# A hybrid decoder layer on one core: the columns in use found from sums of the picks' weights on GpSimd, in place of count products on TensorE

## The chip, the core and the metric

One core of a Trainium2 chip. Its engines run side by side, each through its own queue in program order: TensorE (PE, with the loading of weights listed as PEld), VectorE (DVE), ScalarE (ACT), GpSimd (POOL) and SyncE (SP), which here only issues transfers. The metric is the time of one execution on the device in microseconds (us), the median of the runs. One more execution was recorded by the hardware profiler; every row of a trace comes from that one.

## What is computed

A decoder layer on 256 tokens of width 1024: two attention mixers, their merge, and behind them the part that matters here, a PEER channel mixer. For every token it scores 128 + 128 keys in each of 8 heads, picks the best 16 pairs of a head, and so 128 of 16384 experts with softmax weights. Cut to this part:

```
s = einsum('thcd,cnd->thcn', q, subkeys)          # q = norm(x) @ w_q
s1, i1 = top_k(s[:, :, 0], 16); s2, i2 = top_k(s[:, :, 1], 16)
sc, ci = top_k((s1[..., :, None] + s2[..., None, :]).reshape(T, H, 256), 16)
idx = i1[ci // 16] * 128 + i2[ci % 16];  g = softmax(sc)
a = einsum('td,thkd->thk', x, u[idx])
out = einsum('thk,thkd->td', gelu(a) * g, v[idx])
```

## The kernel before

The kernel does not gather rows of u. It lays the 16384 experts out as 128 columns of 128 experts (partition p, column e) and multiplies all of them with the tokens, column by column; the products of one column are a tile of 128 experts by 256 tokens, and the table of all columns is A (`A1`, `A2`). Then it multiplies A by the softmax weights, of which all but the picked ones are zero, and multiplies the result with v.

**The stage of u.** A loop over e from 0 to 127 takes one column a step. `take()` issues the weights' load (four raw buffers), ScalarE rounds a tile to its high part (`hi_to`, L141) and VectorE subtracts that to get the low part (`lo_to`, L149); both run two or three columns ahead. TensorE does 24 products (`mm3`, L175 to L177), three for each of eight pieces. After every second column `u_evac` applies the GELU on ScalarE (L1091, L1094); where the weights of some tokens stand in A already, its result goes to a work buffer `w0`, and GpSimd multiplies it into A (L1096). At the end of every step `vector_work` does a piece of side work. First that is `select`, the top-k on VectorE. When that is done, it is the groups: `RATE` is 1.15, so a step does one group of four tokens, and about every seventh step two.

**A group** is spread over three steps by `groups_step`. `one_hots` makes on VectorE a one-hot of the pick's partition (L1037, named oh), a one-hot of its column (L1037, eq), and the latter times the weight in two 16-bit parts (L1039). Two groups later `gate_mm` multiplies them on TensorE: for each of four tokens two products into the gate tile `gp` in PSUM (L1047) and one more, the count product, into `used` (L1048), which stays in PSUM over all 64 groups and sums up the high parts of the weights of every expert, apart for tokens 0 to 127 and 128 to 255. A step later `gate_evac` takes the gates out of PSUM: for columns that have their products already VectorE multiplies them into A (L1077, one input in PSUM, one in SBUF), for the others ScalarE copies them to A (L1079), behind VectorE's part since both write A.

**Behind the groups** `lists` runs in small pieces of `yield`ed cost beside the last columns. L1137 makes a flag of every expert in `used` (sum above zero); the flags are sorted into a list of up to 98 slots a partition, by VectorE's max and replace operations on the first level, 32 small matmuls (L1173), and a second level. The indices (L1179) drive the gathers of v's rows and of A's rows on GpSimd (L1284) in the last stage (`v_mm`, L1267). Finished columns of A go to memory through SP (`a_write`, L1056), which the gathers wait for. If the list has no room, a flag makes a branch at the end do the rest.

Order: each engine does its instructions in the order in which the program writes them; TensorE, VectorE, ScalarE and GpSimd wait for each other through the tiles they share. Tiles of one name share a ring of buffers (`w0` has two).

Of the kernel before, what the change touches and what calls it, by code (L numbers as in the profile page):

```python
# [9 lines left out]
F32 = mybir.dt.float32  # L10
F32R = mybir.dt.float32r
BF16 = mybir.dt.bfloat16
# [3 lines left out]
AF = mybir.ActivationFunctionType  # L16
OP = mybir.AluOpType
AX = mybir.AxisListType
PSUM = bass.MemoryType.PSUM

S, D, HD = 256, 1024, 64
KT = D // 128
NT = S // 128
# [4 lines left out]
NH, NK, TOPK = 8, 128, 16  # L28
# [22 lines left out]
NW = NK - ND  # L51
# [51 lines left out]
def tile_hybrid_nsa_dilated_peer(ctx, tc, x, win, wgate, consts, gains, gcols, n1g, n2g, pe, w1, w2, wun, wud, wo, wq, subk,  # L103
                                 cpos, pu, pv, out):
    nc = tc.nc
# [4 lines left out]
    RAW, GT = 4, 4  # L110
# [187 lines left out]
    hT = norm_T(work, x1, g1, None, first_split, psQ, "S")  # L298
    tok = lambda T, k, t: (T[0][:, k, t * 128:(t + 1) * 128], T[1][:, k, t * 128:(t + 1) * 128])

# [93 lines left out]
    def rope(q4, at, bt, nh, np_):  # L394

        T = q4.shape[1]
        a = work.tile([128, T, nh, 16], F32, name="ra")
        b = work.tile([128, T, nh, 16], F32, name="rb")
        a, b = a[:np_], b[:np_]
        bc = lambda z: z.unsqueeze(2).to_broadcast([np_, T, nh, z.shape[-1]])  # L400
        nc.gpsimd.tensor_tensor(a, q4[:, :, :, 0:16], bc(at), op=OP.mult)
# [283 lines left out]
    for t in range(NT):  # L685
        for g in range(3):
            for par in range(2):
                dil_units.append(Unit(
                    ("d%d" % g, t), t, [par, par + 2], 4, {"dq%d" % g, "dk%d" % g, "dv%d" % g},
                    lambda h, g=g: dqT[hrow(h), g, h // 2, :], lambda h, g=g: dkT[hrow(h), g, h // 2, :],  # L690
                    lambda h, k, g=g: vD[:, k, g, h * 64:h * 64 + 64],
# [155 lines left out]
    octx.close()  # L847
    gctx = ExitStack()
    psG = gctx.enter_context(tc.tile_pool(name="psG", bufs=1, space=PSUM))

    used = psG.tile([128, NT, NK], F32, name="used")
    mctx.close()


# [5 lines left out]
    tp_ = ctx.enter_context(tc.tile_pool(name="tp", bufs=2))  # L860
    iotah = tp_.tile([128, NK], F16, name="iotah", bufs=1)

    zero = tp_.tile([128, 2 * S], F32, name="w0")
    nc.gpsimd.memset(zero[0:1], 0.0)
    for o in range(0, ad.shape[1], 2 * S):
# [16 lines left out]
    def Ae(e, n, t0=0, t1=S):  # L882
        return A1[:, e:e + n, t0:t1] if e < 96 else A2[0][:, e - 96:e - 96 + n, t0:t1]
# [8 lines left out]
    for h in range(0, NH, 2):  # L892
        p = psP.tile([128, 2, S], F32, name="pj")
# [131 lines left out]

    prog = {"T": 0, "C": 0}

# [13 lines left out]
        return o1, o2  # L1041

    def gate_mm(t0, oh):
        p = psG.tile([128, GT, NK], F32, name="gp", bufs=3)
        for j in range(GT):
            for i in range(2):
                nc.tensor.matmul(p[:, j, :], oh[0][:, j, :], oh[1][:, j, i, :], start=(i == 0), stop=(i == 1))  # L1047
            nc.tensor.matmul(used[:, t0 // 128, :NW], oh[0][:, j, :], oh[1][:, j, 0, :NW], start=(t0 == 0 and j == 0),  # L1048
                             stop=(t0 == S - GT and j == GT - 1), skip_group_check=True)
        return p  # L1050

    writes = []
# [1 line left out]
    def a_write(e, n, t0, t1):  # L1054
        def f():
            nc.sync.dma_start(ad[e * 128:(e + n) * 128, D + t0:D + t1].rearrange("(e p) t -> p e t", p=128), Ae(e, n, t0, t1))  # L1056
        writes.append((n * (t1 - t0) // 2, f))
# [11 lines left out]
    def gate_evac(t0, p):  # L1069

        pt = p.rearrange("p t e -> p e t")
        C = prog["C"]
        for lo_, hi_ in ((0, 96), (96, 128)):
            m = min(max(C, lo_), hi_)
            if m > lo_:
                av = Ae(lo_, m - lo_, t0, t0 + GT)
                nc.vector.scalar_tensor_tensor(av, pt[:, lo_:m, :], 1.0 / GSCALE, av, op0=OP.mult, op1=OP.mult)  # L1077
            if hi_ > m:
                nc.scalar.activation(Ae(m, hi_ - m, t0, t0 + GT), pt[:, m:hi_, :], AF.Copy, scale=1.0 / GSCALE)  # L1079
        T = prog["T"] = t0 + GT  # L1080
        if T % 128 == 0:
            n = 4 if T < S else 6
            for z in ((0, min(C, 96)), (96, min(C, NW))):
                for e in range(*z, n):
                    a_write(e, min(n, z[1] - e), T - 128, T)
# [30 lines left out]
    def groups_step(n):  # L1116

        for _ in range(n):
            ps = [(t0, gate_mm(t0, oh)) for t0, oh in q_oh[:1]] if len(q_oh) == 2 or state.get("end") else []
            if ps:  # L1120
                q_oh.pop(0)
            for t0, p in q_ps:
                gate_evac(t0, p)
            q_ps[:] = ps
            t0 = next(groups, None)
            if t0 is None:
                state["end"] = True
            else:
                q_oh.append((t0, one_hots(t0)))
# [4 lines left out]
    def lists():  # L1134

        fl = tp_.tile([128, NT, NK], F32, name="oh1", bufs=3)
        nc.vector.tensor_scalar(fl[:, :, :NW], used[:, :, :NW], 0.0, None, op0=OP.is_gt)  # L1137
        yield 300
        kk = tp_.tile([128, 2, NK], F32, name="oh1", bufs=3)
        di = tp_.tile([128, 2, 128], F32, name="oh1", bufs=3)  # L1140
        idm = tp_.tile([128, 2, 128], F32, name="eq", bufs=1)
        nc.gpsimd.iota(idm[:, 0, :], pattern=[[128, 128]], base=-int(PAD), channel_multiplier=1,
                       allow_small_or_imprecise_dtypes=True)
        nc.gpsimd.tensor_copy(di, ident.unsqueeze(1).to_broadcast([128, 2, 128]))
        cols = lambda z: z[:, :NW]
        u0, u1, ids = cols(fl[:, 0, :]), cols(fl[:, 1, :]), cols(idm[:, 0, :])
        k, s_ = kk[:, 0, :NW], kk[:, 1, :NW]

        nc.vector.tensor_scalar(k, u0, -2.0, 1.0, op0=OP.mult, op1=OP.add)
        nc.vector.tensor_tensor(k, k, u1, op=OP.mult)  # L1150
        nc.vector.scalar_tensor_tensor(k, u0, 3.0, k, op0=OP.mult, op1=OP.add)
        yield 550
        nc.vector.scalar_tensor_tensor(s_, k, 0.5, ids, op0=OP.is_gt, op1=OP.mult)
        nc.vector.tensor_scalar(k, k, PAD / KEY, KEY, op0=OP.add, op1=OP.mult)
        nc.vector.tensor_tensor(k, k, s_, op=OP.add)
        yield 550
        for level in range(2):

            for a, b in ((0, 64), (64, NW)) if level == 0 else ((0, NW),):
                kp = k[:, a:b]  # L1160
                for r in range(a, b, 8):
                    nc.vector.max(s_[:, r:r + 8], kp)
                    if r + 8 < b:
                        nc.vector.match_replace(out=kp, in_to_replace=s_[:, r:r + 8], in_values=kp, imm_value=PAD)
                    yield 260 + 3.5 * (b - a)
            yield 3500
            if level == 0:

                p = psTr.tile([128, NW], F32, name="tr")
                d2 = di.rearrange("p a b -> p (a b)")  # L1170
                for j in range(16):
                    o = (128 - 5 * j) % 128
                    nc.tensor.matmul(p[:, j:NW:16], d2[:, o:o + 128], s_[:, j:NW:16], start=True, stop=True)  # L1173
                nc.scalar.activation(k, p, AF.Copy)
                yield 2000
        ei = tp_.tile([128, 4, 128], I32, name="eT", bufs=1)
        idx["a"] = ei[:, 0, :]
        nc.vector.tensor_copy(ei[:, 2, :NW], s_)
        nc.vector.tensor_scalar(ei[:, 0, :NW], ei[:, 2, :NW], int(KEY) - 1, None, op0=OP.bitwise_and)  # L1179
        yield 1300  # L1180

        c = fl[:, 0, 0:1]
        nc.vector.tensor_scalar(c, s_[:, CAPC:CAPC + 1], PAD + 0.5, None, op0=OP.is_gt)
        nc.vector.scalar_tensor_tensor(c, s_[:, CAP0:CAP0 + 1], 2.0 * KEY, c, op0=OP.is_ge, op1=OP.add)
        nc.vector.scalar_tensor_tensor(c, s_[:, S1 - 1:S1], 3.0 * KEY, c, op0=OP.is_lt, op1=OP.add)
        yield 2600
        p = psTr.tile([1, 1], F32, name="tr")
        nc.tensor.matmul(p, c, mhalf, start=True, stop=True)
        nc.vector.tensor_scalar(ei[0:1, 3, 0:1], p, -0.25, None, op0=OP.is_lt)
        idx["more"] = ei[0:1, 3, 0:1]  # L1190
        yield 300

    mk = lists()

    def list_work(ns):
# [38 lines left out]
    for e in range(NK):  # L1234
        if e % 2 == 0:
            p = psP.tile([128, 2, S], F32, name="pj")
# [259 lines left out]
```

## Time and profile before

| | us |
|---|---|
| median of 3 runs (975.61 to 978.22) | 975.74 |
| the profiled execution | 977.78 |
| its span, first to last instruction | 975.93 |
| TensorE busy | 955.8 (98%) |
| VectorE busy | 725.5 (74%) |
| ScalarE busy | 501.0 (51%) |
| GpSimd busy | 264.4 (27%) |

Shares over the whole span are averages over stages of different kinds; what a change in one stage is worth is read from that stage. The columns of rows are said in front of each group of them below. In all of them "out<-in" are the names of the program's tiles, and L and a number is the line. A recorded matmul's duration includes its way through the array, and matmuls overlap; VectorE's records overlap their neighbours by some 0.1 us as well.

### The profile page before, as it was taken

The numbers are of one execution on the slowest core, as the hardware profiler recorded it, in microseconds if no ns is written. First come the engines' busy times: TensorE is split into PE (matmuls) and PEld (weight loads), VectorE is DVE, ScalarE is ACT, GpSimd is POOL, SyncE is SP. The second block draws the span as 40 slices with busy tenths as digits, with TensorE's granted clock in tenths as the row PEclk, the third lists the DMA queues.
The fourth block names the chain that finished last, engine by engine and source line by source line (L and its number), as shares of the span: only waits on it lengthen the run. The fifth ranks groups of instructions, "written<-read, shape, count | busy, mean of one in ns | idle before, by whom it ended". The sixth has DMA issues, their size and how long they took to land.

```text
span 975.9 us, 18699 instructions
## 1 busy us (share of the span) xinstructions
PE 955.8 (98%) x7163; PEld 887.0 (91%) x7163; DVE 725.5 (74%) x1471; ACT 501.0 (51%) x866; POOL 264.4 (27%) x272
## 2 busy tenths in 40 slices
PE   9999999999999999998999999999999989999997
PEld 9989898998889999998999999999998868888885
DVE  5587666556667898899888999997664657777775
ACT  6466634444445445445544444434344546766663
POOL 4412224000000141041000011112123867666620
PEclk9999999999999999999999999999899999999999
DMA  8879755559776789888878778856898999999941
GB/s 283 290 249 326 266 173 196 187 202 349 273 247 238 242 306 314 302 301 301 299 259 267 259 196 244 234 166 198 264 302 288 403 409 320 327 327 329 323 148 46
DMA packets 95638, 259.91 MB, mean 266 GB/s; under 512 B 9908, under 2 KB 39221, under 8 KB 95543
## 3 DMA queue, kind: packets, MB, share of 16 engines
q1 hardware_dynamic: 80566, 193.25, 60.0%
q0 software_dynamic: 14112, 64.23, 18.0%
q8 instruction: 58, 0.95, 0.4%
q10 hardware_dynamic: 864, 1.18, 0.4%
q14 instruction: 38, 0.30, 0.1%
HBM read 240.80 MB, written 80.75 MB: 329 GB/s over the span
## 4 chain that ended last, share of the span: by engine, by line
PE 88%; DVE 8%; issue 2%; ACT 1%; POOL 1%; DMA 0%; ACTq 0%; POOLq 0%
PE acc L1267 24%; PE pj L175 17%; PE pj L177 16%; PE pj L176 16%; PE gp L1047 3%; DVE lo L149 3%; PE pv L593 2%; PE S L549 2%; PE used L1048 1%; PE tr L577 1%; PE tr L910 1%; DVE oh L980 1%; PE acc L177 1%; PE acc L175 1%; PE acc L176 1%
## 5 line engine op out<-in xcount | busy, mean ns | idle before, releaser
L175 PE MATMUL pj<-T_h,hi 128*128 128x256 f32 x1104 | 319.0, 289 | 0.5 <-ACT A L1091 0.4
L177 PE MATMUL pj<-T_h,lo 128*128 128x256 f32 x1104 | 313.7, 284 | 2.9 <-DVE lo L149 2.8
L176 PE MATMUL pj<-T_l,hi 128*128 128x256 f32 x1104 | 312.9, 283 | 0.0
L149 DVE TENSOR_TENSOR lo<-raw,hi 128x1024 fp32r<-128x1024 f32 x204 | 259.5, 1275 | 50.0 <-PE pj L177 26.7
L141 ACT ACTIVATE hi<-raw 128x1024 fp32r<-128x1024 f32 x205 | 216.4, 1060 | 156.2 <-PE pj L176 58.2
L177 PEld LDWEIGHTS pj<-T_h,lo 128*128 128x128 f32 x1104 | 212.2, 192 | 4.7 <-DVE lo L149 4.5
L175 PEld LDWEIGHTS pj<-T_h,hi 128*128 128x128 f32 x1104 | 212.3, 192 | 1.9 <-ACT A L1091 0.6
L176 PEld LDWEIGHTS pj<-T_l,hi 128*128 128x128 f32 x1104 | 212.4, 192 | 0.0
L1284 POOL DMA_INDIRECT A<-ad,eT x98 | 131.9, 1346 | 60.3 <-DVE oh L1228 33.1
L1267 PE MATMUL acc<-hi,w 128*128 128x512 f32 x336 | 131.0, 390 | 2.9 <-issue 1.6
L1267 PE MATMUL acc<-lo,w 128*128 128x512 f32 x336 | 130.8, 389 | 0.0
L1267 PE MATMUL acc<-hi,oh 128*128 128x512 f32 x336 | 130.8, 389 | 0.0
L1323 DVE TENSOR_TENSOR lo<-A,hi 128x1024 fp32r<-128x1024 f32 x98 | 119.5, 1219 | 0.0
L1096 POOL TENSOR_TENSOR A<-A,w 128x512 f32<-128x512 f32 (+28 forms) x39 | 39.1, 1003 | 256.2 <-ACT w L1094 256.2
L1290 ACT ACTIVATE hi<-A 128x1024 fp32r<-128x1024 f32 x98 | 102.6, 1047 | 6.2 <-DMA A<-ad,eT 6.2
L175 PE MATMUL pj<-hi,T_h 128*128 128x256 f32 x336 | 97.1, 289 | 0.0
L1228 DVE TENSOR_TENSOR oh<-A,w 128x256 fp32r<-128x256 f32 x106 | 44.8, 423 | 70.3 <-ACT w L1227 62.7
L176 PE MATMUL pj<-lo,T_h 128*128 128x256 f32 x336 | 95.2, 283 | 0.3 <-DVE lo L149 0.3
L177 PE MATMUL pj<-hi,T_l 128*128 128x256 f32 x336 | 95.1, 283 | 0.0
L1227 ACT ACTIVATE w<-A 128x256 fp32r<-128x256 f32 x106 | 44.1, 417 | 77.9 <-PE acc L1267 74.8
L1267 PEld LDWEIGHTS acc<-hi,w 128*128 128x128 f32 x336 | 63.1, 188 | 16.9 <-issue 2.1
L1267 PEld LDWEIGHTS acc<-hi,oh 128*128 128x128 f32 x336 | 63.1, 188 | 13.4 <-DVE oh L1228 0.3
(276 smaller groups left out, 1421.3 us busy)
## 6 DMA issues: line engine op xcount, KB each, us to landing
raw<-in_pu_dram SPq DMA_DIRECT2D x128, 512.0 KB, 4.5
ad<-in_pv_dram SPq DMA_DIRECT2D x120, 512.0 KB, 5.8
raw<-in_win_dram SPq DMA_DIRECT2D x44, 512.0 KB, 4.5
ad<-A SPq DMA_DIRECT2D x27, 256.0 KB, 4.9
ad<-A SPq DMA_DIRECT2D x17, 384.0 KB, 6.0
raw<-in_w_dram SPq DMA_DIRECT2D x8, 512.0 KB, 4.4
raw<-in_wo_dram SPq DMA_DIRECT2D x8, 512.0 KB, 5.2
raw<-in_wq_dram SPq DMA_DIRECT2D x8, 512.0 KB, 4.5
```

The costliest lines, as they stand in the source:

```text
L141: nc.scalar.activation(split[i], raws[i], AF.Copy)
L149: nc.vector.tensor_tensor(lo, raws.pop(i), split[i], op=OP.subtract)
L175: nc.tensor.matmul(ps, s_[0], m_[0], start=first, stop=False, skip_group_check=True)
L176: nc.tensor.matmul(ps, s_[0], m_[1], start=False, stop=False, skip_group_check=True)
L177: nc.tensor.matmul(ps, s_[1], m_[0], start=False, stop=last, skip_group_check=True)
L1096: nc.gpsimd.tensor_tensor(av, av, tmp[:, :, :T], op=OP.mult)
L1227: nc.scalar.activation(wh, a, AF.Copy)
L1228: nc.vector.tensor_tensor(wl, a, wh, op=OP.subtract)
L1267: nc.tensor.matmul(acc[t][d], w[w_][:, ts_], v[v_][:, d * 512:(d + 1) * 512], start=(t, d) not in begun, stop=last and n == 2, skip_group_ ...
L1284: nc.gpsimd.indirect_dma_start(out=b, out_offset=None, in_=ad, in_offset=bass.IndirectOffsetOnAxis(ap=idx["a"][:, s_:s_ + 1], axis=0))
L1290: nc.scalar.activation(hi, raw, AF.Copy)
L1323: nc.vector.tensor_tensor(lo, v_of(n_lo), his[n_lo], op=OP.subtract)
```

## The change

The count products go, and the tile `used` moves from PSUM to SBUF as 16-bit numbers, two for each partition and column, cleared by GpSimd. The gates' tile gets a fourth buffer in PSUM. In `gate_evac` ScalarE copies the 120 columns of the four tokens from PSUM to a 16-bit tile (from the `w0` ring), and GpSimd adds it to `used`, two tokens at a time. `lists` reduces the two sums of an expert to their larger one, and compares that with zero.

```diff
-    used = psG.tile([128, NT, NK], F32, name="used")
...
+    used = tp_.tile([128, NT, NW, 2], BF16, name="used", bufs=1)
+    nc.gpsimd.memset(used, 0.0)
     zero = tp_.tile([128, 2 * S], F32, name="w0")
...
     def gate_mm(t0, oh):
-        p = psG.tile([128, GT, NK], F32, name="gp", bufs=3)
+        p = psG.tile([128, GT, NK], F32, name="gp", bufs=4)
         for j in range(GT):
             for i in range(2):
                 nc.tensor.matmul(p[:, j, :], oh[0][:, j, :], oh[1][:, j, i, :], start=(i == 0), stop=(i == 1))
-            nc.tensor.matmul(used[:, t0 // 128, :NW], oh[0][:, j, :], oh[1][:, j, 0, :NW], start=(t0 == 0 and j == 0),
-                             stop=(t0 == S - GT and j == GT - 1), skip_group_check=True)
         return p
...
             if hi_ > m:
                 nc.scalar.activation(Ae(m, hi_ - m, t0, t0 + GT), pt[:, m:hi_, :], AF.Copy, scale=1.0 / GSCALE)
+        g = tp_.tile([128, NW, GT], BF16, name="w0")
+        nc.scalar.activation(g, pt[:, :NW, :], AF.Copy)
+        for j in range(0, GT, 2):
+            nc.gpsimd.tensor_tensor(used[:, t0 // 128], used[:, t0 // 128], g[:, :, j:j + 2], op=OP.add)
...
         fl = tp_.tile([128, NT, NK], F32, name="oh1", bufs=3)
-        nc.vector.tensor_scalar(fl[:, :, :NW], used[:, :, :NW], 0.0, None, op0=OP.is_gt)
+        nc.vector.tensor_reduce(fl[:, :, :NW], used, op=OP.max, axis=AX.X)
+        yield 1100
+        nc.vector.tensor_scalar(fl[:, :, :NW], fl[:, :, :NW], 0.0, None, op0=OP.is_gt)
         yield 300
```

## Rows read from the trace of the kernel before

**Rows 1.** The page, part 4: share of each engine in the chain that ended last.

```profile
PE 88%; DVE 8%; issue 2%; ACT 1%; POOL 1%; DMA 0%; ACTq 0%; POOLq 0%
```

**Rows 2.** Windows: length, busy us (count) of PE, PEld, DVE, ACT, POOL; clock, DMA, GB/s.

```profile
463.00:668.00 205.00, 205.00 (x2101) 202.59 (x2101) 185.61 (x315) 97.36 (x227) 23.14 (x28) 1.00 0.77 239
610.00:659.00 49.00, 49.00 (x502) 48.40 (x502) 47.24 (x80) 21.23 (x47) 8.19 (x7) 1.00 0.69 199
784.00:795.00 11.00, 8.07 (x34) 5.88 (x33) 4.21 (x6) 3.99 (x6) 6.87 (x6) 1.00 1.02 413
```

**Rows 3.** Tiles used and gp: duration ns min/median/max, first and last start.

```profile
L1048 PE MATMUL used<-oh,oh x256: 216/216/216, 463.3 to 666.8; 128*128 128x120 f16 x128
...
L1047 PE MATMUL gp<-oh,oh x512: 219/219/230, 463.2 to 666.7; 128*128 128x128 f16 x171
```

**Rows 4.** Timeline of PE, one token of a group: start us, duration us.

```profile
647.64 0.22 PE L1048 MATMUL used<-oh,oh 128*128 128x120 f16 x1
...
647.80 0.22 PE L1048 MATMUL used<-oh,oh 128*128 128x120 f16 x1
```

**Rows 5.** Groups by form, ACT, 463 to 668 us: busy us, mean ns, idle before.

```profile
L1094 ACT ACTIVATE w<-pj 128x488 f32<-128x488 f32 x1 | 0.6, 581 | 0.0
```

**Rows 6.** Waits, 463 to 668 us: who waited for whom, us in total, times, longest.

```profile
ACT A L1079 <- DVE A L1077: 65.6, 62, 2.7
```

**Rows 7.** Groups by form, POOL, 463 to 676 us: busy us, mean ns, idle before.

```profile
L1096 POOL TENSOR_TENSOR A<-A,w 128x8 f32<-128x8 f32 x1 | 0.2, 206 | 22.6 <-ACT w L1094 22.6
...
L1096 POOL TENSOR_TENSOR A<-A,w 128x248 f32<-128x248 f32 x1 | 0.7, 717 | 6.0 <-ACT w L1094 6.0
...
L1096 POOL TENSOR_TENSOR A<-A,w 128x504 f32<-128x504 f32 x1 | 1.3, 1277 | 5.1 <-ACT w L1094 5.1
...
L1144 POOL COPY oh<-ident 128x256 f32<-128x256 f32 x1 | 0.4, 396 | 0.0
```

**Rows 8.** Timeline of POOL and DVE around 645.7 us.

```profile
645.73 1.16 POOL L1096 TENSOR_TENSOR A<-A,w 128x448 f32<-128x448 f32 x1 [6.07 <-ACT w L1094]
...
645.32 0.63 DVE L1077 SCALAR_TENSOR_TENSOR A<-gp,A 128x384 f32<-128x384 f32 x2
645.86 1.30 DVE L1037 TENSOR_TENSOR oh<-iotah,eT 128x512 f16<-128x512 f16 x1
```

**Rows 9.** Groups by form, DVE, 463 to 668 us: busy us, mean ns, idle before.

```profile
L149 DVE TENSOR_TENSOR lo<-raw,hi 128x1024 fp32r<-128x1024 f32 x56 | 68.4, 1221 | 10.2 <-PE pj L177 8.2 <-issue 1.9
L1039 DVE TENSOR_TENSOR oh<-eq,gT 128x1024 f16<-128x1024 f16 x62 | 42.9, 692 | 2.1
L1037 DVE TENSOR_TENSOR oh<-iotah,eT 128x512 f16<-128x512 f16 x62 | 34.3, 554 | 0.0
L1037 DVE TENSOR_TENSOR eq<-iotah,eT 128x512 f16<-128x512 f16 x62 | 25.8, 416 | 0.0
```

**Rows 10.** Timeline of DVE and POOL around 145.4 us.

```profile
145.24 1.22 DVE L149 TENSOR_TENSOR lo<-raw,hi 128x1024 fp32r<-128x1024 f32 x1
146.37 1.76 DVE L417 TENSOR_TENSOR qn<-s,hr 128x512 f32<-128x512 f32 x1
...
145.40 2.17 POOL L631 TENSOR_TENSOR yN<-yN,ytmp 128x512 f32<-128x512 f32 x1 [5.49 <-DVE ytmp L630]
```

**Rows 11.** Timeline of POOL and DVE, 351 to 356.5 us.

```profile
351.77 3.72 POOL L982 TENSOR_TENSOR oh<-oh,code 128x256 f32<-128x256 f32 x2 [6.18 <-DVE oh L980]
...
352.28 1.77 DVE L149 TENSOR_TENSOR lo<-raw,hi 128x1024 fp32r<-128x1024 f32 x1
...
356.00 0.81 DVE L986 TENSOR_REDUCE ef<-oh 128x32 f32<-128x640 f32 x1
```

**Rows 12.** Timeline of DVE and POOL at 718 and 750 us; line L864.

```profile
718.37 0.22 DVE L1179 TENSOR_SCALAR eT<-eT 128x120 int32<-128x120 int32 x1
...
749.81 1.34 POOL L1284 DMA_INDIRECT A<-ad,eT  x1 [7.94 <-DMA A<-x1d]
...
L864 POOL MEMSET w<- x1: 518/518/518, 275.4 to 275.4; 1x512 f32 x1
```

## The prediction

> **What bounds the kernel now.** I read the chain of waits first: 88% of it is TensorE [rows 1]. The engine is not waiting for anything in particular; its own products are the time. Then I cut out the stretch that the change touches, from the first count product at 463 us to the last at 667 us, and asked for the busy time of every engine in it [rows 2]. The reader should see three numbers there. TensorE is busy 205.00 of 205 us, at the full granted clock. VectorE is busy 185.61 us, and in the late part (610 to 659 us) 47.24 of 49 us: it is nearly as full as TensorE. ScalarE has 97.36 us and GpSimd 23.14 us. So TensorE sets the pace, and a second limit lies 19 us behind it on average and under 2 us behind it at the end. That second limit is what this forecast turns on.
>
> **The removed products.** The stretch has 256 count products beside 512 gate products [rows 3]. Their recorded 216 ns is latency, not cost. In the order of time one token (two gate products and a count product) takes from 647.64 to 647.80, 0.16 us for three products of almost equal width [rows 4], so one costs 53 ns, and 256 of them 13.6 us. If TensorE stays the bound, the stretch goes from 205.0 to 191.4 us.
>
> **The added copy on ScalarE.** 64 copies of 128x480 from PSUM. The nearest row is a 128x488 activation from PSUM, 581 ns [rows 5]; I take 0.57 us, 36.5 us in all. ScalarE would have 97.4 + 36.5 = 134 of some 200 us. Queued behind each copy is the next split of a weight tile into its high part (L141), for which VectorE's low part waits; ScalarE today stands 65.6 us in this stretch waiting for VectorE's product L1077 [rows 6], and that idle time hides the copy. I cost it at nothing; without the cover it would be at most the 0.57 us a group, 36 us.
>
> **The added sums on GpSimd.** 128 adds of 240 elements in place. The trace has no add on 16-bit operands. The nearest rows are the same operation in f32: 206 ns for 8 elements and 717 ns for 248 [rows 7], 2.13 ns an element, so 0.70 us for 240 and 90 us in all. From below, a one-input copy of 256 elements took 0.40 us [rows 7], so 0.38 us. I take 0.70, the row of the same operation with two inputs, and keep 0.38. GpSimd itself has room (23 + 90 of 205 us).
>
> **What the sums do to VectorE.** This is the step that decides. At 645.73 a GpSimd multiply runs for 1.16 us. VectorE's product L1077, one of whose inputs lies in PSUM, runs beside it at its usual length; the one-hot compare behind it (both inputs in SBUF) starts at 645.86 and is recorded with 1.30 us instead of the 0.42 us that the same compare takes alone [rows 8, 9]. It ended at 647.16, so it began its 0.42 us at 646.74, 0.15 us ahead of the multiply's recorded end. The two engines exclude each other: a VectorE product with two inputs in SBUF stands still while a GpSimd operation runs. Two more places tell who gets the next turn. At 145.40 GpSimd waits behind L149, and although VectorE's next product is queued directly behind that, GpSimd goes first: its add took 2.17 us, and L417 behind it 1.76 us [rows 10]. At 351.77 two GpSimd multiplies stand in a row, and L149 got in between them, with 1.77 us instead of 1.22 [rows 11]. So they take turns.
>
> Now the turns of one group. VectorE's order is L149, L1077, compare, compare, multiply L1039. The copy stands on ScalarE behind L1079, which waits for L1077, so the first add is ready about 1 us after L1077 ends, during L1039. It takes the turn behind L1039 and holds L149 for 0.70 - 0.15 = 0.55 us. The second add takes the turn behind L149 and so runs beside L1077, which it does not hold. Only in the groups that follow one of the 28 multiplies L1096 [rows 2] is GpSimd one operation late, and the second add holds a product as well; with 1.15 groups a step that is every second group.
> - First adds: 64 x 0.55 = 35.2 us. Second adds: 32 x 0.55 = 17.6 us.
> - L1096 today hides part of itself beside L149 and L1077: the held first compares have 34.3 us against 25.8 us for the second ones [rows 9], so it costs VectorE 8.5 us. Its 28 operations have 8 to 504 elements, 256 on average, so by [rows 7] about 21 us of their own and 17 us of lock (less 28 x 0.15); pushed back by the adds I let it hold in full, 8.5 us more.
>
> VectorE's need in the stretch is 185.6 + 35.2 + 17.6 + 8.5 = 246.9 us, and 2 us for its small gaps: 249 us. That is 58 us above TensorE's 191.4, so VectorE is the new bound and the 13.6 us are not collected. The stretch grows by 249 - 205 = 44 us.
>
> The page "SBUF — State Buffer" of the Trainium skill (Who interferes with whom) has the same lock, between a GpSimd operation that reads SBUF and a VectorE one with two SBUF inputs, but held for the whole instruction. By that an add would hold 0.70 us and L1096 its full 21 us, and the sum would be 185.6 + 44.8 + 22.4 + 12.5 + 2 = 267 us, 18 us more than mine. The trace agrees with the lock and shows it released 0.15 us early [rows 8].
>
> **Edits that cost nothing.** A fourth buffer for the gate products takes the bank of the counts: TensorE never stands still here [rows 2], so nothing is gained. The cleared tile is one more memset on GpSimd between two stages, about the 0.52 us of the one beside it [rows 12], on an engine that is idle there; the load queue's zero row waits that long behind it, covered by four raw buffers. SP's writes of finished columns wait for L1096, later by one or two adds, with the same cover. The list starts with a reduce over 480 elements (under the 0.81 us of one over 640 [rows 11]) in place of a compare, and waits for the last add; its first matmuls are queued half a step later. The indices were ready at 718.4 us and the first gather ran at 749.8 us, held by a DMA [rows 12], so 31 us cover it; uncovered it would be 1.5 us.
>
> **The sum.** The profiled execution took 977.78 us (a span of 975.93 and 1.85 around it), 2.04 us above the median of the three runs. 977.8 + 44 = 1021.8; less 2.0 to stand against the median, **1020 us**. Bounds: adds of 0.38 us hold 0.23 us, so 96 x 0.23 + 8.5 = 31 us, a stretch of 218 and 989 us; with second adds and L1096 always hidden 64 x 0.23 = 15 us, 973 us. If no add ever finds L1077 (128 x 0.55 + 8.5 = 79 us) the stretch is 267, 1038 us; with 0.70 us of lock each 128 x 0.70 + 12.5 = 102 us, 290 and 1061 us.
>
> **The rivals.**
> - TensorE stays the bound (faster): the adds cost VectorE less than the 191.4 - 185.6 = 5.8 us it has to spare. Then 13.6 us come off: 962 us. For it: TensorE is at 100%. Against it: products are held at each place where the two engines meet [rows 8, 10, 11], and 5.8 us over 128 adds is 45 ns each. It decides below that price. Chance 0.10.
> - Cheap 16-bit adds, 0.38 us: 973 to 989 us, for which only the copy's row speaks. Chance 0.13.
> - Long holds: every add holds a product, or ScalarE comes to wait for the two shared work buffers that GpSimd has not yet read and its splits come late: 1038 to 1061 us and above. For it: the buffers are shared with the activations of L1094. Against it: the turns alternate [rows 11]. Chance 0.12. By the Trainium skill's rule of the whole instruction, named above, the time lies in this case too.
> - TensorE's granted clock falls because the engine now pauses 58 us in the stretch. TensorE was busy 8.07 of 11 us from 784 to 795 us and kept 1.00, its 2.4 GHz level [rows 2]. I give it no chance of its own; it would lie in the case above.
> - It does not do what it says: sums above zero pick other columns than the counts did, and the fallback branch at the end runs. The same weights stand in both, so 0.03, slower.
>
> **How the numbers follow.** The forecast has 0.62, with a range of its own from 1000 to 1045 us. A measurement of this kernel can tell about 0.3%, 3 us. Faster: 0.10 and 0.02 of the cheap case; same: 0.04 of it; slower: the rest, 0.84. The range from 975 to 1055 us leaves out the first rival and a bit of the cheap case below, and the dearer part of long holds above.
>
> **What would show it.** In the profile after: 64 copies near 0.57 us on ScalarE, 128 adds near 0.70 us of their own on GpSimd and longer where they wait; L149 or L1039 recorded longer than 1.22 and 0.69 us; TensorE idle in the stretch with VectorE as its releaser; the stretch near 249 us and everything behind it unchanged in length. I am wrong if L149 keeps 1.22 us throughout, if the adds take 0.3 us, or if TensorE is still busy all the time.

## The result, and the profile after

The changed kernel takes 1000.22 us (median of 6 runs, 998.01 to 1003.8) where the kernel before takes 975.67 us (6 runs, 972.66 to 978.22). The ratio is 1.0253, with an interval from 1.0235 to 1.0271: 24.5 us slower. The prediction had 1020 us, a range from 975 to 1055 us, and 0.84 on slower. The direction and the mechanism came out; the size, 44 us, is nearly twice what was measured.

The profiled execution of the changed kernel has a span of 996.1 us, 20.2 us over the 975.9 us of before. (It lies 2.2 us under its kernel's median and the one of before 2.1 us over its own, which makes the 24.5 us of the medians.) Where the 20.2 us are is read from three stretches, cut at the first and the last gate product:

| stretch | before | after | difference |
|---|---|---|---|
| to the first gate product | 463.2 us | 464.8 us | +1.6 |
| first to last gate product | 203.5 us | 220.1 us | +16.6 |
| from there to the end | 309.2 us | 311.2 us | +2.0 |

The chain of waits of the changed kernel, which answers to [rows 1], has lost TensorE's near monopoly:

```profile
PE 65%; DVE 25%; issue 5%; POOL 2%; ACT 1%; DMA 0%; DVEq 0%; ACTq 0%; POOLq 0%
```

The windows of the changed kernel, with the columns of [rows 2], show why:

```profile
464.70:686.20 221.50, 201.84 (x1845) 196.78 (x1844) 219.36 (x311) 118.89 (x284) 154.04 (x149) 0.96 0.71 215
635.00:686.00 51.00, 43.60 (x385) 42.29 (x385) 50.55 (x74) 23.70 (x55) 34.83 (x33) 0.93 0.53 151
```

VectorE is busy 219.36 of 221.5 us. Before it was TensorE that had no gap; now TensorE stands some 20 us. In the late part VectorE is busy 50.55 of 51 us. For whom TensorE and ScalarE wait from 464 to 690 us (us in total, times, longest) shows the same:

```profile
PE gp L1048 <- DVE oh L1040: 17.3, 8, 3.4
PE pj L177 <- DVE lo L149: 2.2, 5, 0.7
...
ACT A L1078 <- DVE A L1076: 101.1, 62, 3.1
```

TensorE stands for VectorE's one-hots and low parts. ScalarE stands for VectorE as well; no wait of it for GpSimd, with which it shares the work buffers, is recorded there. The bound has moved, as the prediction said.

The tiles of the changed kernel give the gate products and the two new operations (columns as in [rows 3]):

```profile
L1048 PE MATMUL gp<-oh,oh x512: 216/219/315, 464.8 to 684.9; 128*128 128x128 f16 x171
...
L1080 ACT ACTIVATE w<-gp x64: 565/578/580, 467.7 to 692.5; 128x480 bf16<-128x480 f32 x64
...
L1082 POOL TENSOR_TENSOR used<-used,w x128: 644/972/1628, 468.3 to 694.3; 128x240 bf16<-128x240 bf16 x128
```

The copy takes 0.578 us (0.57 forecast). An add that finds nothing in its way takes 0.644 us (0.70 forecast); the median add is recorded with 0.972 us, since it also waits its turn behind VectorE. What the adds do to VectorE stands in its groups by form, from 464 to 690 us, which answer to [rows 9]:

```profile
L149 DVE TENSOR_TENSOR lo<-raw,hi 128x1024 fp32r<-128x1024 f32 x57 | 94.4, 1656 | 0.0
L1040 DVE TENSOR_TENSOR oh<-eq,gT 128x1024 f16<-128x1024 f16 x62 | 50.8, 820 | 2.1
L1038 DVE TENSOR_TENSOR eq<-iotah,eT 128x512 f16<-128x512 f16 x62 | 38.6, 623 | 0.0
L1038 DVE TENSOR_TENSOR oh<-iotah,eT 128x512 f16<-128x512 f16 x62 | 29.2, 471 | 0.0
```

The products do the same work in both kernels, so whatever is recorded beyond their usual length [rows 9] is time in which they were held. L149: 94.4 - 57 x 1.22 = 24.9 us. L1040: 50.8 - 42.9 = 7.9 us. The two compares: 38.6 - 25.8 = 12.8 and 29.2 - 25.8 = 3.4 us. That is 49.0 us; before, the same account gave 34.3 - 25.8 = 8.5 us. **The adds cost VectorE 40.5 us**, for which the prediction had 61.3.

Which operation held which product can be read too. A held product does its usual length at the end of its record, so its work began that much before its end; and each time one GpSimd operation ends 0.13 to 0.15 us after that point. Sorted by that operation, the held time is:

| held by | before | after | forecast for after |
|---|---|---|---|
| first add of a group | | 60 times, 23.6 us | 64 times, 35.2 us |
| second add | | 44 times, 12.7 us | 32 times, 17.6 us |
| multiply of the u loop | 20 times, 8.5 us | 24 times, 12.9 us | 17.0 us |

One group in the order of time, VectorE first and then GpSimd (start us, duration us), shows the case that the prediction described, a first add that holds L149:

```profile
611.46 0.41 DVE L1038 TENSOR_TENSOR eq<-iotah,eT 128x512 f16<-128x512 f16 x1
611.90 0.69 DVE L1040 TENSOR_TENSOR oh<-eq,gT 128x1024 f16<-128x1024 f16 x1
612.51 1.67 DVE L149 TENSOR_TENSOR lo<-raw,hi 128x1024 fp32r<-128x1024 f32 x1
614.10 0.51 DVE L1076 SCALAR_TENSOR_TENSOR A<-gp,A 128x352 f32<-128x352 f32 x1
...
612.21 2.47 POOL L1082 TENSOR_TENSOR used<-used,w 128x240 bf16<-128x240 bf16 x2 [2.52 <-ACT w L1080]
```

The pair of adds begins at 612.21, during L1040. The first gets its turn behind it and holds L149 for 1.67 - 1.22 = 0.45 us. The second waits behind L149 and runs beside L1076, which has an input in PSUM and keeps its 0.51 us. The pair takes 2.47 us, though its own work is 1.3. Of the first adds 34 hold L149 in this way, 0.45 us each. Another 23 hold L1040, for 0.34 us, and in 19 groups it is the second add that holds L149; the second adds also reach into the first compare 21 times, for 0.12 us each.

### The profile page after: what moved, and what is told of

Read it like the earlier page. It is cut to its first block, busy times and chain, and to the rows that moved or that the text cites. A ratio compares the mean times of both kernels' runs of the same rounds, so it can differ in the third digit from the quotient of the medians.

```text
span 996.1 us, 18462 instructions
## 1 busy us (share of the span) xinstructions
PE 955.8 (96%) x6907; PEld 882.6 (89%) x6907; DVE 763.0 (77%) x1472; ACT 526.4 (53%) x930; POOL 400.4 (40%) x401
## 4 chain that ended last, share of the span: by engine, by line
PE 65%; DVE 25%; issue 5%; POOL 2%; ACT 1%; DMA 0%; DVEq 0%; ACTq 0%; POOLq 0%
PE acc L1272 23%; DVE lo L149 11%; PE pj L175 10%; PE pj L177 10%; PE pj L176 10%; DVE eq L1038 3%; DVE A L1076 2%; DVE oh L1038 2%; PE pv L593 2%; PE S L549 2%; DVE oh L1040 1%; PE tr L577 1%; POOL used L1082 1%; PE tr L911 1%; DVE oh L981 1%
## 5 line engine op out<-in xcount | busy, mean ns | idle before, releaser
L177 PE MATMUL pj<-T_h,lo 128*128 128x256 f32 x1104 | 318.6, 289 | 8.0 <-DVE lo L149 7.8
L175 PE MATMUL pj<-T_h,hi 128*128 128x256 f32 x1104 | 323.5, 293 | 0.5 <-ACT A L1094 0.4
L176 PE MATMUL pj<-T_l,hi 128*128 128x256 f32 x1104 | 316.8, 287 | 0.0
L149 DVE TENSOR_TENSOR lo<-raw,hi 128x1024 fp32r<-128x1024 f32 x204 | 282.4, 1387 | 39.2 <-PE pj L177 15.5
L177 PEld LDWEIGHTS pj<-T_h,lo 128*128 128x128 f32 x1104 | 216.0, 196 | 11.6 <-DVE lo L149 11.5
L175 PEld LDWEIGHTS pj<-T_h,hi 128*128 128x128 f32 x1104 | 216.3, 196 | 2.0 <-ACT A L1094 0.6
L176 PEld LDWEIGHTS pj<-T_l,hi 128*128 128x128 f32 x1104 | 216.6, 196 | 0.0
L1082 POOL TENSOR_TENSOR used<-used,w 128x240 bf16<-128x240 bf16 x128 | 136.1, 1063 | 84.8 <-ACT w L1080 79.1
L1289 POOL DMA_INDIRECT A<-ad,eT x98 | 129.2, 1318 | 61.3 <-DVE oh L1233 33.8
L1078 ACT ACTIVATE A<-gp 128x112 f32<-128x112 f32 (+22 forms) x116 | 24.8, 261 | 103.2 <-DVE A L1076 101.1
```

The source lines that it names most:

```text
L149: nc.vector.tensor_tensor(lo, raws.pop(i), split[i], op=OP.subtract)
L175: nc.tensor.matmul(ps, s_[0], m_[0], start=first, stop=False, skip_group_check=True)
L176: nc.tensor.matmul(ps, s_[0], m_[1], start=False, stop=False, skip_group_check=True)
L177: nc.tensor.matmul(ps, s_[1], m_[0], start=False, stop=last, skip_group_check=True)
L1082: nc.gpsimd.tensor_tensor(used[:, t0 // 128], used[:, t0 // 128], g[:, :, j:j + 2], op=OP.add)
L1289: nc.gpsimd.indirect_dma_start(out=b, out_offset=None, in_=ad, in_offset=bass.IndirectOffsetOnAxis(ap=idx["a"][:, s_:s_ + 1], axis=0))
```

## The experiments

Three kernels ran on one chip with the kernel before at 983.99 us (its runs there scatter from 973.9 to 989.2 us), three more on a chip with 975.63 us, the last two with 975.96 us. Where a difference is small, the stretch from the first to the last gate product is compared, which repeats within 0.1 us in the three kernels here that leave TensorE as the bound without count products.

**The copies alone.** The kernel before, with the 64 copies on ScalarE and nothing that reads them.

```diff
+        g = tp_.tile([128, NW, GT], BF16, name="w0")
+        nc.scalar.activation(g, pt[:, :NW, :], AF.Copy)
```

> The kernel before, with ScalarE's 64 copies added and nothing that reads them: the count products stay, GpSimd adds nothing. My theory (GpSimd's adds hold VectorE's products) expects the time of before, 976 us within 3, with L149 at 1.22 us and TensorE busy all through the stretch. The rival that ScalarE's queue or the shared work buffers made the change slow expects 985 to 1000 us, with L149 waiting for L141.

Measured: 983.74 us (10 runs), ratio 1.0013, interval 0.9969 to 1.0058. In its profile (ScalarE's and VectorE's groups, then the whole stretch)

```profile
L1081 ACT ACTIVATE w<-gp 128x480 bf16<-128x480 f32 x63 | 36.2, 575 | 0.0
...
L149 DVE TENSOR_TENSOR lo<-raw,hi 128x1024 fp32r<-128x1024 f32 x57 | 69.6, 1221 | 10.2 <-PE pj L177 8.1 <-issue 1.9
...
464.00:670.00 206.00, 206.00 (x2106) 203.63 (x2103) 185.17 (x314) 126.16 (x292) 21.28 (x30) 1.00 0.77 237
```

The expected 976 us belong to a chip on which the kernel before takes that; here it takes 983.99 us, and the time is the same as before's. 36.2 us of copies are there, TensorE still has no gap and L149 keeps 1.221 us. The stretch is 203.6 us against 203.5. The copies cost nothing, and a rival by which ScalarE's queue delays the splits falls. Work buffers that wait for GpSimd's reading are not tested here; for them the waits of the changed kernel above speak, which have none of ScalarE for GpSimd.

**Both ways at once.** The kernel before keeps its count products and their use, and also makes the copies and the adds into a tile that nothing reads.

```diff
+    sums = tp_.tile([128, NT, NW, 2], BF16, name="sums", bufs=1)
+    nc.gpsimd.memset(sums, 0.0)
...
+        g = tp_.tile([128, NW, GT], BF16, name="w0")
+        nc.scalar.activation(g, pt[:, :NW, :], AF.Copy)
+        for j in range(0, GT, 2):
+            nc.gpsimd.tensor_tensor(sums[:, t0 // 128], sums[:, t0 // 128], g[:, :, j:j + 2], op=OP.add)
```

> The kernel before, count products and all, with the copies and GpSimd's 128 adds beside them into a tile that nothing uses. If VectorE with its held products sets the pace of the stretch (221 us against TensorE's 205 with the count products), the time is that of the changed kernel, 1000 us within 4: the removal of the count products is worth nothing there. The rival that their removal still pays its 13.6 us inside the changed kernel expects 1014 us.

Measured: 1000.79 us (4 runs), ratio 1.0187, interval 1.011 to 1.0264. That is the expected time, but on the chip where the kernel before takes 983.99 us; the interval holds the changed kernel's 1.0253 and is wide, so the stretch has to decide. The tile of the gate products and the stretch:

```profile
L1049 PE MATMUL gp<-oh,oh x512: 219/219/314, 464.9 to 686.3; 128*128 128x128 f16 x171
...
464.90:687.60 222.70, 210.84 (x2100) 207.11 (x2099) 219.07 (x310) 119.95 (x285) 155.63 (x150) 0.98 0.70 215
```

With 256 count products more than the changed kernel the stretch is 686.3 - 464.9 = 221.4 us against 220.1: their removal is worth 1.3 us once VectorE is the bound, not 13.6. VectorE's busy time is the same (219.07 and 219.36 us). The rival's 13.6 us more would be 233.7 us. From the last gate product to the end this execution took 4.5 us more than the changed kernel; that is not explained here.

**Neither.** The changed kernel without the copies and the adds; the columns in use are a fixed pattern of as many flags.

```diff
+    nc.gpsimd.memset(used[:, 0, 0:CAP0], 1.0)
+    nc.gpsimd.memset(used[:, 1, S1:CAPC], 1.0)
...
-        g = tp_.tile([128, NW, GT], BF16, name="w0")
-        nc.scalar.activation(g, pt[:, :NW, :], AF.Copy)
-        for j in range(0, GT, 2):
-            nc.gpsimd.tensor_tensor(used[:, t0 // 128], used[:, t0 // 128], g[:, :, j:j + 2], op=OP.add)
```

> The changed kernel without copies and adds: the sums are left out, and the flags are a fixed pattern that fills the same slots, so the gathers are as many. This shows what the removal of the count products is worth alone. By my sum TensorE stays the bound and 13.6 us come off: 962 us. The rival that VectorE, 47.24 of 49 us busy late in the stretch, takes over there expects about half of it, 967 to 970 us.

Measured: 972.0 us (10 runs), ratio 0.9892, interval 0.9846 to 0.9938. The stretch has the length that the prediction gave to a TensorE that stays the bound: 657.1 - 467.2 = 189.9 us, and 203.5 - 13.6 = 189.9. In its profiled execution 8 us of that were missing at the end, where the last stage waited for gathers, so the kernel ran once more, beside another run of before:

> The kernel without counts, copies and adds once more: its first profile had the stretch at 190 us and lost 8 us later, where TensorE waited for gathers in the last stage. If that loss belongs to the kernel (the gathers start earlier against the same transfers), TensorE waits there again and the time is about 976 us; if it was that one execution, the tail behind the last gate product is 309 us as before, and the time 962 to 966 us.

Measured: 968.08 us (975.96 for before). The tile of its gate products:

```profile
L1050 PE MATMUL gp<-oh,oh x512: 219/219/229, 467.2 to 657.1; 128*128 128x128 f16 x171
```

The stretch is again 189.9 us, and what follows takes 966.2 - 657.1 = 309.1 us, as in the kernel before (309.2). So the 8 us are not lost in every execution. Of the ten runs, five lie between 964.5 and 969.6 us and five between 974.4 and 978.4; where the others of the slower half lost their time was not recorded. The first gate product comes 4.0 us later than before, in both profiled executions: TensorE's granted clock was 0.89 from 20 to 60 us there and 1.00 in the kernel before, with TensorE busy 39.1 of 40 us in either. That takes 4.0 of the 13.6 us; the span is 9.7 us shorter than the profiled one of before (966.2 and 975.9 us). Against the run of before beside it, which was itself 1.7 us shorter than the profiled one, 7.9 us are left.

Both halves of the change are now priced apart. Taking the products away is worth 13.6 us of the stretch by itself. Adding copies and adds costs 221.4 - 203.5 = 17.9 us in the stretch where the products stay, and 220.1 - 189.9 = 30.2 us where they are gone.

**One long add for each group.** Is it the number of GpSimd's operations that costs? All four positions are summed by one add of 480 elements. The sums of the two halves of the tokens are merged, because a second set of sums of this width leaves too little room in SBUF for a later stage, and the flags are fixed.

```diff
-    used = tp_.tile([128, NT, NW, 2], BF16, name="used", bufs=1)
+    used = tp_.tile([128, NW, GT], BF16, name="used", bufs=1)
...
-        for j in range(0, GT, 2):
-            nc.gpsimd.tensor_tensor(used[:, t0 // 128], used[:, t0 // 128], g[:, :, j:j + 2], op=OP.add)
+        nc.gpsimd.tensor_tensor(used, used, g, op=OP.add)
```

> The changed kernel with one GpSimd add of 480 elements a group in place of two of 240 (about 64 x 1.10 = 70 us of GpSimd's own time against 128 x 0.64 = 82), the flags a fixed pattern, so nothing waits for the sums. If the engines take turns and a product is held as long as the add in front of it lasts, L149 is held for some 0.9 us a group in place of 0.45 and nothing hides beside L1076: the stretch from the first to the last gate product grows from 220 us to 235 to 245. If GpSimd's total time decides, it shrinks by 12 us, to 208.

**Two adds again, in that same frame,** to have the pair's price with the list's new start out of the way. Here an add's target is two of every four elements of a row of sums.

```diff
-        nc.gpsimd.tensor_tensor(used, used, g, op=OP.add)
+        for j in range(0, GT, 2):
+            nc.gpsimd.tensor_tensor(used[:, :, j:j + 2], used[:, :, j:j + 2], g[:, :, j:j + 2], op=OP.add)
```

> The pair to the run with one add: two adds of 240 elements a group, with the same fixed flags. The stretch should be that of the changed kernel, 220 us within 2, since the flags and the list lie behind it.

Measured: 1003.67 and 1004.72 us, one run each (975.63 for before). The tiles and VectorE's groups of the kernel with one add:

```profile
L1048 PE MATMUL gp<-oh,oh x512: 216/219/314, 466.3 to 694.2; 128*128 128x128 f16 x171
...
L1081 POOL TENSOR_TENSOR used<-used,w x64: 1088/1312/1682, 469.8 to 702.4; 128x480 bf16<-128x480 bf16 x64
...
L149 DVE TENSOR_TENSOR lo<-raw,hi 128x1024 fp32r<-128x1024 f32 x54 | 103.9, 1924 | 0.0
L1038 DVE TENSOR_TENSOR eq<-iotah,eT 128x512 f16<-128x512 f16 x62 | 25.6, 413 | 0.0
```

and of the kernel with two:

```profile
L1048 PE MATMUL gp<-oh,oh x512: 216/219/314, 467.9 to 694.3; 128*128 128x128 f16 x171
...
L1082 POOL TENSOR_TENSOR used<-used,w x128: 689/1132/1697, 471.4 to 704.1; 128x240 bf16<-128x240 bf16 x128
...
L149 DVE TENSOR_TENSOR lo<-raw,hi 128x1024 fp32r<-128x1024 f32 x55 | 93.3, 1696 | 0.0
L1038 DVE TENSOR_TENSOR eq<-iotah,eT 128x512 f16<-128x512 f16 x62 | 38.9, 627 | 0.0
```

Both expectations missed, and usefully. One add of 480 has 64 x 1.088 = 70 us of its own, two of 240 have 128 x 0.689 = 88 us, yet the stretches are 227.9 and 226.4 us. The rows of VectorE are of 464 to 690 us. The long add holds L149 more (103.9 - 54 x 1.22 = 38.0 us against 26.2) and the compare eq not at all (25.6 us, against 38.9). Over the four products and up to the last gate product, 4 us later, the products are held 56.5 us with the long add and 54.7 with the two short ones, worked out as for the changed kernel above. So neither GpSimd's busy time nor the number of its operations sets the stretch; the time in which VectorE's products are held comes out alike, and so does the stretch. The short adds here are slower than in the changed kernel, 0.689 against 0.644 us, with only the layout of their target changed. A first add holds L149 for 0.51 us here and for 0.45 in the changed kernel; 128 x 0.045 = 5.8 us is near the 6.3 us between the stretches (226.4 and 220.1).

This pair also bears on the end of the changed kernel. With fixed flags the list does not wait for the adds, and what follows the last gate product takes 1002.8 - 694.3 = 308.5 us, where the changed kernel has 311.2. With one execution each this is a hint: the two executions of the kernel that leaves out both differ by 10 us there (319.5 and 309.1).

**GpSimd as busy, but reading nothing.** Copies and adds are gone, the flags are fixed, and GpSimd clears a buffer from the ring of work buffers twice in each group.

```diff
-        g = tp_.tile([128, NW, GT], BF16, name="w0")
-        nc.scalar.activation(g, pt[:, :NW, :], AF.Copy)
-        for j in range(0, GT, 2):
-            nc.gpsimd.tensor_tensor(used[:, t0 // 128], used[:, t0 // 128], g[:, :, j:j + 2], op=OP.add)
+        for j in range(2):
+            junk = tp_.tile([128, 640], BF16, name="w0")
+            nc.gpsimd.memset(junk, 0.0)
```

> The kernel without count products, copies and adds (flags a fixed pattern), with 128 memsets of 640 16-bit elements on GpSimd where the adds stood, some 0.6 us each into the ring of work buffers: GpSimd is about as busy as with the adds, but reads nothing. If products are held by GpSimd's reading, L149 stays at 1.22 us and the stretch at the 190 us of the run without counts. If any GpSimd work beside VectorE slows it, or GpSimd's busy time as such, the stretch is near 220 us again.

Measured: 962.04 us (975.96 for before). The stretch, the cleared tile, and four clears of it beside VectorE's products in the order of time:

```profile
463.50:654.20 190.70, 190.70 (x1837) 188.34 (x1836) 182.19 (x315) 96.16 (x225) 94.07 (x149) 1.00 0.82 256
...
L1079 POOL MEMSET w<- x128: 621/631/644, 448.9 to 659.2; 128x640 bf16 x128
...
604.97 0.69 DVE L1038 TENSOR_TENSOR oh<-eq,gT 128x1024 f16<-128x1024 f16 x1
605.58 1.22 DVE L149 TENSOR_TENSOR lo<-raw,hi 128x1024 fp32r<-128x1024 f32 x1
...
604.26 2.34 POOL L1079 MEMSET w<- 128x640 bf16 x4
```

From 604.26 to 606.60 GpSimd runs without a pause, and the multiply L1038 and L149 begin beside it and keep 0.69 and 1.22 us. A clear takes 0.631 us, as long as an add, and there are as many. GpSimd is busy 94.07 of 190.7 us and no clear holds a product; what is held is held by the multiplies of the u loop, 20 times and 6.7 us, as in the kernel that leaves out both. TensorE has no gap, and the gate products take 189.8 us from first to last, as there. So it is not that GpSimd runs, nor that it writes: what the adds do and the clears do not is to read SBUF.

**Flags on VectorE, four to a word.** If the adds hold VectorE for 40 us, a small operation on VectorE itself should be cheaper. ScalarE writes its copy in an 8-bit float format, so that a column's four weights, none of them negative, fill one 32-bit word. VectorE takes the maximum of that word and the words so far, one operation of 120 elements for each group, placed at the start of the next group's work. A weight that rounds to zero in the 8-bit format makes no flag.

```diff
-    used = tp_.tile([128, NT, NW, 2], BF16, name="used", bufs=1)
+    used = tp_.tile([128, NT, NW], I32, name="used", bufs=1)
...
+    def fold():
+        while last:
+            h, v = last.pop()
+            nc.vector.tensor_tensor(used[:, h], used[:, h], v, op=OP.max)
...
     def gate_evac(t0, p):
...
+        fold()
...
+        g = tp_.tile([128, NW, GT], mybir.dt.float8e5, name="w0")
+        nc.scalar.activation(g, pt[:, :NW, :], AF.Copy, saturate=False)
+        last.append((t0 // 128, g.rearrange("p e t -> p (e t)").bitcast(I32)))
...
+        nc.vector.tensor_scalar(fl[:, :, :NW], used, 0.0, None, op0=OP.is_gt)
```

> A version without GpSimd: ScalarE copies the gates of four tokens as four 8-bit floats, which make one 32-bit integer, and VectorE keeps the larger of it and of a running one, 120 elements a group, one group late. A VectorE product of 128x120 took 0.28 us, some 0.2 us of its queue, so VectorE's need is 185 + 64 x 0.2 = 198 us, above TensorE's 190 and below the 204 of before. My theory expects a stretch of 196 to 202 us and a time of 968 to 975 us, some 0.3% faster than before. If the copies or a busier VectorE cost more than counted, 976 us or above.

Measured: 970.83 us (11 runs), ratio 0.9937, interval 0.9919 to 0.9955: 0.6% faster than the kernel before. The tile of its gate products, the stretch, and VectorE's groups:

```profile
L1049 PE MATMUL gp<-oh,oh x512: 218/219/230, 466.2 to 659.2; 128*128 128x128 f16 x171
...
463.00:662.00 199.00, 196.17 (x1884) 193.59 (x1883) 194.85 (x377) 121.53 (x287) 21.06 (x27) 1.00 0.79 248
...
L149 DVE TENSOR_TENSOR lo<-raw,hi 128x1024 fp32r<-128x1024 f32 x57 | 69.5, 1219 | 0.8 <-PE pj L177 0.5
L1072 DVE TENSOR_TENSOR used<-used,w 128x120 int32<-128x120 int32 x61 | 22.5, 369 | 0.0
```

The time was met and the stretch missed, 193.0 us against 196 to 202. 61 maxima are recorded with 22.5 us of VectorE and L149 is back at 1.22 us. The two engines are now level, 196.17 and 194.85 of 199 us, and the stretch is 193.0 us, 10.5 us under the kernel before and 3.1 us over the one that leaves the flags out. Of those 10.5 us the whole kernel keeps some 5: the first gate product comes 3.0 us later, where TensorE's granted clock was 0.97 from 60 to 160 us and the kernel before had 1.00, and what follows the last one takes 2.3 us more (311.5 and 309.2 us).

## Why the prediction was right in direction and too high in size

**What bounds the kernel, and what would bound it next: right.** TensorE bound the stretch, VectorE came next, and VectorE bounds the changed kernel at 219.36 of 221.5 us.

**The removed products, 53 ns each, 13.6 us: right to a tenth.** The kernel that leaves out both parts has 189.9 us. That they would not be collected was right as well: 1.3 us of 13.6 between the kernel with both ways at once and the changed one.

**The copies at nothing: right.** The kernel with the copies alone has a ratio of 1.0013 and a stretch 0.1 us longer.

**The lock: right in kind.** L149 is held by the adds, GpSimd's turn comes behind VectorE's running product, and the product with an input in PSUM runs beside an add. As many clears, which read nothing, hold nothing. The Trainium skill, page "SBUF — State Buffer", section "Who interferes with whom", says the same: a VectorE instruction with two SBUF inputs contends with a GpSimd instruction that reads SBUF, and not with one that only writes it. The Trainium skill's further rule, on the same page in its section "SBUF: two separate sides", that the lock lasts the whole instruction, which the prediction weighed at 18 us more, does not hold to the letter here: an add with 0.644 us of its own held L149 for 0.45 us, and in every hold the product began 0.13 to 0.15 us ahead of the GpSimd operation's recorded end.

**The step that failed is the turns of one group**, the 61.3 us in the sum of VectorE's need. They measured 40.5. How often an add holds a product was near the forecast, 104 times against 96; the length of a hold was not, 0.35 us on average against 0.55:
- First adds, forecast at 64 x 0.55 = 35.2 us, all on L149, held products 60 times for 23.6 us, 0.39 us each. The price of 0.70 us came from f32 rows at 2.13 ns an element; the 16-bit add takes 0.644. On L149 a hold was 0.45 us, and 23 of the first adds held L1040, for 0.34 us. A step of the u loop has one L149 and 1.15 groups, so not every first add can find one.
- Second adds, forecast at 32 x 0.55 = 17.6 us, held products 44 times for 12.7 us. So they hold more often than in every second group, and for less: 0.44 us in the 19 cases on L149, but 0.12 us where they only reach into the first compare.
- The multiplies of the u loop, forecast at 8.5 us more, cost 12.9 - 8.5 = 4.4 us more.

With 40.5 us the prediction's own sum gives 185.6 + 40.5 + 2 = 228 us for VectorE, and the stretch is shorter. Counted strictly from the first to the last gate product, VectorE is busy 184.1 of 203.5 us before and 218.0 of 220.1 us after, 33.8 us more. The holds in there make 39.4 us. Against them stand two L149 fewer (54 and 56, 2.4 us) and shorter products L1076 (2.0 us): by the last gate product VectorE had made 182 low parts before and 180 after, so it had used up part of its lead over TensorE, and that work came later. The records overlap by 1.7 us more as well. That leaves 33.3 us, within 0.5 us of the measured difference.

**Edits that cost nothing: one did cost.** The prediction let the list's start hide under the 31 us until the first gather. Its cover was the wrong one, since the first to stand is TensorE, for L149. The list's reduce waits for the last adds, which come late because GpSimd takes its turns to the end, and L149 is queued behind the reduce on VectorE. The end of the stretch in the changed kernel, GpSimd, then VectorE, then TensorE:

```profile
686.78 5.64 POOL L1082 TENSOR_TENSOR used<-used,w 128x240 bf16<-128x240 bf16 x4
...
693.63 1.37 POOL L1082 TENSOR_TENSOR used<-used,w 128x240 bf16<-128x240 bf16 x2
...
695.03 0.65 DVE L1140 TENSOR_REDUCE oh<-used 128x240 f32<-128x480 bf16 x1 [3.11 <-POOL used L1082]
...
699.02 0.39 PE L177 MATMUL pj<-T_h,lo 128*128 128x256 f32 x1 [1.95 <-DVE lo L149]
...
702.82 0.39 PE L177 MATMUL pj<-T_h,lo 128*128 128x256 f32 x1 [0.66 <-DVE lo L149]
...
706.17 0.39 PE L177 MATMUL pj<-T_h,lo 128*128 128x256 f32 x1 [0.21 <-DVE lo L149]
```

VectorE stands 3.11 us for the adds, and TensorE then 1.95 + 0.66 + 0.21 = 2.8 us for L149. The kernel before has no such wait. How much of the 2.8 us is the reduce is not shown: 2.2 us of the same wait stand in the kernel with both ways, whose list reads the count products, and in the one with flags on VectorE, which has no adds; with fixed flags it is 1.0 and 1.6 us. All of these are kernels in which VectorE has used up part of its lead, and the kernels that leave TensorE without a gap in the stretch have no such wait. The part behind the change is 2.0 us longer than before, which is less than single executions of one kernel differ by there.

**The rivals.** TensorE staying the bound would have needed adds that cost VectorE under 5.8 us; they cost 40.5. The cheap case (0.38 us an add, 973 to 989 us) and the case of long holds (1038 us and above) both fell: an add is near the f32 rate, and the hold is shorter than it, not longer. No wait of ScalarE for GpSimd is recorded in the stretch, so the shared work buffers did not cost either.

## What to carry to other kernels

Work moved to a GpSimd that stands idle is not free where VectorE is almost as full as the bound: each GpSimd operation that reads SBUF can stop a VectorE product with two inputs in SBUF for most of its own length (0.45 of 0.644 us on L149), so count held time against the margin of the second-fullest engine before moving anything. Here the margin was 5.8 us and the holds 40.5. A smaller operation on the full engine itself (22.5 us with four weights packed in a word) was the cheaper place. An engine's lead over the bound is part of that margin: where it is used up, the bound starts to wait, here also behind the changed stretch.

## What the runs showed of the hardware that was not expected

- The time of a GpSimd add on 16-bit operands depends on the layout of its target (the shortest records of each): 0.644 us for 240 contiguous elements, 0.689 us where the target is two of every four. One add of 480 elements takes 1.088 us, not twice 0.644.
- 128 clears by GpSimd, 0.631 us each, ran beside VectorE's products without holding one, while as many adds of the same length cost VectorE 40.5 us.
- The end of a hold is sharp: the product's work began 0.13 to 0.15 us before the recorded end of the GpSimd operation in all holds of the kernels before and after, whether that was a 16-bit add or an f32 multiply.
- TensorE's granted clock was 0.93, a mean between its two levels of 1.2 and 2.4 GHz, from 635 to 686 us of the changed kernel, where TensorE was busy 43.6 of 51 us; in that part of the program the kernels without a gap had 1.00. The prediction gave this no chance. TensorE was busy 200.4 us in the stretch, against 189.9 for the same products without the adds; what that cost the kernel was not separated, since VectorE was the bound there. A gap is not the only thing that goes with a lower clock: in the kernel before it was 0.92 in the 30 us behind the last gate product, where TensorE was busy all the time.
- The part ahead of the change varies by some us between kernels with the same products there: the first gate product began at 463.2 us before, at 464.8 after, and at up to 467.9 us in the experiments. Where it came late, the granted clock had been lower: 0.96 from 20 to 60 us in the changed kernel, 0.89 there where both parts are left out, 0.97 from 60 to 160 us with flags on VectorE. The kernel before and the one with the copies alone, which began at 463.2 and 463.4 us, had 1.00 in both windows. TensorE's busy time from 20 to 60 us was 39.1 us in all of them, and why the clock fell is open.
